# Up projection of a gated MLP: both token parts in one 512-column matmul, seven PSUM banks a tile, sums made during the products

## The chip, the cores and the metric
The kernel runs on one core of a Trainium2 chip. The metric is the time of one execution in microseconds, as the median of three runs. Engines are named as in the profile: PE multiplies matrices and writes PSUM (eight banks of 512 fp32 columns), PEld is its weight load, DVE is the vector engine, ACT the scalar engine, POOL GpSimd, SP the queue that issues most transfers.

## The reference
A decoder layer on 512 tokens of 2048 columns: layer norm, an input projection with four groups of attention heads, an output projection, a residual with layer norm, and a gated MLP. The change lies in the MLP's first half:
```python
def conv_ffn(x, w_up, conv_w, conv_b, w_down):      # x (1, 512, 2048), w_up (2048, 11264)
    S = x.shape[1]
    u, g = jnp.split(x @ w_up, 2, axis=-1)          # 5632 columns each
    gp = jnp.pad(g, ((0, 0), (CONV_WIDTH - 1, 0), (0, 0)))
    gc = conv_b
    for tap in range(CONV_WIDTH):                   # causal, width 3, along the tokens
        gc = gc + conv_w[tap] * gp[:, tap:tap + S]
    return (jax.nn.gelu(gc) * u) @ w_down
...
    h = layer_norm(DEEPNORM_ALPHA * h + mix, ln1_g[l], ln1_b[l])
    ffn = conv_ffn(h, ffn_w_up[l], ffn_conv_w[l], ffn_conv_b[l], ffn_w_down[l])
    h = layer_norm(DEEPNORM_ALPHA * h + ffn, ln2_g[l], ln2_b[l])
```

## The kernel before
Every fp32 matrix product is made of fp32r matmuls: an operand is split into a high part (a rounded copy) and a low part (what is left), and three matmuls add high x high, high x low and low x high (`PARTS`).

The up projection takes 44 tiles `f`. A tile is 128 columns of `u` and the same 128 of `g` for all 512 tokens. It is computed as a product of 2x2 blocks with seven products instead of eight (Strassen-Winograd): the blocks of the weights are halves of the 2048 rows and `u` or `g`, those of the tokens are halves of the rows and the two halves of 256 tokens. `UP` lists for each of the seven products the bank, the half of the bank, the weight operand `iw` and the token operand `ix`. A tile's rows come in two units `u` of four blocks of 128, so a unit is 7 x 4 x 3 = 84 matmuls of 256 columns.

The token operands are made once, at the stage's start, in `up_half0`, `up_half1` and `up_sums`, for eight blocks `kp`, and stay in SBUF: `xo[kp][part][ix]`. `up_first` computes tile 0 in plain form beside that.

The weight operands of a unit are made in `weight_operands`, at high precedence (an offset of 900 instructions): SP loads the blocks (`wr`), ACT makes the high parts `wh` and a negated copy in `wl`, a transfer on POOL's queue adds the weights to `wl` in memory (L926), POOL makes the four sums `S` (L934 to L937), ACT and DVE split them into `ws` (L899, L900). `wh` and `wl` have two buffers, `S` two, `ws` 12, the temporaries `t` 36. Each engine works its queue in order; the order is fixed when the program is built.

`ffn_up(f, u, n)` runs one unit of tile `f`, as its first (n = 0) or second (n = 1). The tile holds four PSUM banks (`bank4`; tags "g" with three banks and "a" with five): products 1 and 4 share a bank, 3 and 5, 2 and 6. After the second unit `up_finish` adds up: ACT copies product 0, DVE makes six adds (L996 to L1002). `gated` then does the convolution (one ACT step L1010, two DVE steps L1011 and L1013), the GELU on ACT (L1015) and the multiplication with `u` (L1016, on POOL), and every second tile `set_aside` makes token sums on POOL for the down projection and stores them. `step_aside` is called once per unit.

The order of the products is 0 to 6 from tile 5 on; in the first tiles the products with sums of tokens come last. The last two tiles run their units in another order (`up_sequence`). In tiles 2 to 17 `up_residual` takes one of 16 blocks of the residual a tile: a load, two DVE steps, a store (L1053 to L1057).

Of the kernel before, what the change touches and what calls it, by code (L numbers as in the profile page):

```python
# [11 lines left out]
F32 = mybir.dt.float32  # L12
F32R = mybir.dt.float32r
AF = mybir.ActivationFunctionType
# [3 lines left out]
P = 128  # L18
# [6 lines left out]
FT = DFF // P  # L25
# [16 lines left out]
class Trunk:  # L42
# [774 lines left out]
    def up_half0(self, kp):  # L817
        nc = self.nc
        e = self.up_blocks(kp, 0, "g")
        o = self.pT.tile([P, 2, 512], F32R, tag="T", name="x0")  # L820
        nc.gpsimd.tensor_scalar(o[:, 0], e, 1.0, 0.0, op0=ALU.mult, op1=ALU.add)
        nc.vector.tensor_sub(o[:, 1], e, o[:, 0].bitcast(F32))
        self.e0.append(e)
        self.xo.append([[o[:, p, :256], o[:, p, 256:]] for p in range(2)])

    def up_half1(self, kp):

        nc = self.nc
        e1 = self.up_blocks(kp, 1, "a")
        x12, x22 = (self.tmp(nm, (P, 2, 256), F32R) for nm in ("x12", "x22"))  # L830
        for i, x in enumerate((x12, x22)):
            e = e1[:, i * 256:(i + 1) * 256]
            nc.gpsimd.tensor_scalar(x[:, 0], e, 1.0, 0.0, op0=ALU.mult, op1=ALU.add)
            nc.vector.tensor_sub(x[:, 1], e, x[:, 0].bitcast(F32))
        self.x12.append(x12)
        self.e1.append(e1)
        for p in range(2):
            self.xo[kp][p].append(x22[:, p])

    def up_sums(self, kp):  # L840
        nc = self.nc
        e0, e1 = self.e0[kp], self.e1[kp]
        b11, b21, b12, b22 = e0[:, :256], e0[:, 256:], e1[:, :256], e1[:, 256:]
        tt = self.pP.tile([P, 4, 256], F32, tag="P", name="tt")
        nc.vector.tensor_sub(tt[:, 0], b12, b11)
        nc.gpsimd.tensor_sub(tt[:, 2], b22, b12)
        nc.vector.tensor_sub(tt[:, 1], b22, tt[:, 0])
        nc.gpsimd.tensor_sub(tt[:, 3], b21, tt[:, 1])
        if kp < 4:
            xt = [self.pT.tile([P, 4, 256], F32R, tag="T", name="xt") for _ in range(2)]  # L850
            xt = [[x[:, i:i + 2] for x in xt] for i in (0, 2)]
        else:
            xt = [[self.tmp("xt", (P, 2, 256), F32R) for _ in range(2)] for _ in range(2)]
        for i in range(2):
            nc.scalar.copy(xt[i][0], tt[:, 2 * i:2 * i + 2])
            nc.vector.tensor_sub(xt[i][1], tt[:, 2 * i:2 * i + 2], xt[i][0].bitcast(F32))
        for p in range(2):
            self.xo[kp][p] += [xt[i // 2][p][:, i % 2] for i in range(4)]

    def up_first(self):  # L860


        nc = self.nc
        ps = [self.bank("g", "up") for _ in range(2)]
        ws = [self.next_unit(), self.next_unit()]
        self.x12, self.e1 = [], []

        def products(u, half, k):
            kp = 4 * u + k
            x1 = ([self.xo[kp][p][0] for p in range(2)] if half == 0  # L870
                  else [self.x12[kp][:, p] for p in range(2)])
            x2 = [self.xo[kp][p][1 + half] for p in range(2)]
            for g, iw, x in ((0, 0, x1), (1, 3, x1), (0, 1, x2), (1, 2, x2)):
                for i, j in self.PARTS:
                    nc.tensor.matmul(
                        ps[g][:, half * 256:(half + 1) * 256],
                        ws[u][iw][i][:, k * P:(k + 1) * P], x[j],
                        start=(half == 0 and kp == 0 and iw in (0, 3) and (i, j) == (0, 0)),
                        stop=(kp == 7 and iw in (1, 2) and (i, j) == (1, 0)),
                        skip_group_check=True)  # L880

        for k in range(4):
            products(0, 0, k)
        for k in range(4):
            products(1, 0, k)
            self.up_half1(k)
        for k in range(4):
            products(0, 1, k)
            self.up_half1(4 + k)
        for kp in range(4):  # L890
            self.up_sums(kp)
        for k in range(4):
            products(1, 1, k)
            self.up_sums(4 + k)
        return ps
# [61 lines left out]
    def up_product(self, bk, w, u, i, opens, last):  # L957
        b, half, iw, ix = self.UP[i]
        ps = bk[b][:, half * 256:(half + 1) * 256]
        for k in range(4):  # L960
            x = self.xo[4 * u + k]
            for i, j in self.PARTS:
                self.nc.tensor.matmul(  # L963
                    ps, w[iw][i][:, k * P:(k + 1) * P], x[j][ix],
                    start=(opens and k == 0 and (i, j) == (0, 0)),
                    stop=(last and k == 3 and (i, j) == (1, 0)), skip_group_check=True)

    def ffn_up(self, f, u, n):

        if n == 0:  # L970
            self.bk[f] = self.bank4(f % 2 == 0, "up"), set()
        bk, opened = self.bk[f]
        w = self.next_unit()


        late = max(0, 5 - f) if u == 0 else int(f == 1)
        for i in (*range(3, 3 + late), 0, 1, 2, *range(3 + late, 7)):
            b = self.UP[i][0]
            self.up_product(bk, w, u, i, b not in opened, n == 1)
            opened.add(b)  # L980
        self.step_aside()
        if (f, n) == (FT - 1, 0):
            for kp in range(4):
                self.hidden_operands(kp)
        if n == 1:
            self.up_finish(f, self.bk.pop(f)[0])

    def up_finish(self, f, bk):
        nc = self.nc
# [15 lines left out]
    def gated(self, f, g, up):  # L1005

        nc = self.nc
        c = self.tmp("c")
        cw = lambda k: self.prm[:, C_CW + 44 * k + f:C_CW + 44 * k + f + 1]
        nc.scalar.activation(c, g, AF.Identity, bias=self.prm[:, C_CB + f:C_CB + f + 1], scale=cw(2))  # L1010
        nc.vector.scalar_tensor_tensor(c[:, 1:], g[:, :511], cw(1), c[:, 1:], op0=ALU.mult,  # L1011
                                       op1=ALU.add)
        nc.vector.scalar_tensor_tensor(c[:, 2:], g[:, :510], cw(0), c[:, 2:], op0=ALU.mult,  # L1013
                                       op1=ALU.add)
        nc.scalar.activation(c, c, AF.Gelu_apprx_tanh)  # L1015
        (nc.vector if f == 0 else nc.gpsimd).tensor_mul(c, c, up)  # L1016
        c = c.rearrange("p (a n) -> p a n", a=2)
        if f % 2 == 0:
            self.b1 = c
        else:  # L1020
            self.aside.append(self.set_aside(self.b1, c))
# [147 lines left out]
    def ffn(self):  # L1169
        nc = self.nc  # L1170
# [3 lines left out]
        for f, u in self.up_sequence():  # L1174
            n = int(f in seen)
            seen.add(f)
            if f > 0:
                self.ffn_up(f, u, n)
            elif n:
                self.gated(f, *self.up_first())  # L1180
            if n and 2 <= f < 18:
                self.up_residual(f - 2)
        self.st2 = [self.cst.tile([P, 4, 6], F32, name=f"st2_{t}") for t in range(NT)]
        self.due = deque((4, 5))
        acc = []
# [1 line left out]
        for c, k0, nk in self.CHUNKS:  # L1187
            sets = self.column_sets(c)
            for q in sets:
                bk = [self.bank("g" if i < 3 else "a", "dn") for i in range(7)]  # L1190
                nu = nk // 2
                for u in range(nu):
                    w = self.next_unit()
# [26 lines left out]
        for f in range(2, 4):  # L1220
            h, l = self.load_unit(self.wtail[f])
# [3 lines left out]
        for t in range(NT):  # L1225
            ps = self.bank("g" if t else "a", "dt")
            for f in range(8):
                x = self.ho[18 + f // 2][((0, 7), (1, 2))[f % 2][t // 2]]
                for j, p in self.PARTS:
                    nc.tensor.matmul(ps, x[j][:, t % 2 * P:(t % 2 + 1) * P], tail[f][p],  # L1230
                                     start=(f == 0 and (j, p) == (0, 0)),
                                     stop=(f == 7 and (j, p) == (1, 0)))
# [155 lines left out]
```

## Time and profile before
| | |
|---|---|
| median of 3 runs | 2337.31 us (2329.66 to 2339.68) |
| the profiled execution: its time, its span | 2341.35 us, 2339.6 us |
| PE, PEld busy in the span | 2232.7 us (95%), 2083.5 us (89%) |
| DVE, ACT, POOL busy | 1591.7 us (68%), 1229.5 us (53%), 1368.4 us (58%) |
| matmuls | 15454 |
| matmuls of up at L963, first and last start | 917.4 to 1829.3 us |
| granted clock of PE, mean | 0.983 of full speed |

Busy is the time in which an engine works on at least one instruction. Matmuls overlap: one of 256 columns lasts 283 ns in the profile, but the next begins before it ends, so the spacing of starts tells the pace. Idle time of an engine is put down to what released it ("<-").

### The profile page before, as it was taken

The page shows a single profiled execution, that of the slowest core. Times are in us where ns is not written, and L with a number is a line of the kernel's source. Part 1 is how long each engine was busy: PE and PEld are TensorE (multiplying, and loading weights), DVE is VectorE, ACT ScalarE, POOL GpSimd, SP SyncE. Part 2 cuts the span into 40 slices and gives each one's busy share as a digit, 9 for nine tenths or more (in the row PEclk, how much of TensorE's full clock was granted, in tenths as well). Part 3 has the DMA queues.
Part 4 walks back from the last instruction along what each step waited for, and adds up shares of the span by engine and source line. Part 5 has one row for each costly group of instructions (what it writes and reads, how often), then busy time and mean ns, then how long its engine had stood idle before and what let it go on. Part 6 is the DMA issues. An engine that isn't in the chain of part 4 may idle for free. (4 is left out here: it accounts for less than half of the span.)

```text
span 2339.6 us, 40306 instructions
## 1 busy us (share of the span) xinstructions
PE 2232.7 (95%) x15454; PEld 2083.5 (89%) x15454; DVE 1591.7 (68%) x2204; ACT 1229.5 (53%) x2129; POOL 1368.4 (58%) x1197
## 2 busy tenths in 40 slices
PE   7999999999999998899999999999999899999995
PEld 6788888888888878899999999999999899899994
DVE  7544455456675348687787767777676878677778
ACT  5444453355563135565555555565555666565651
POOL 5212110123234517787887878877777687777874
PEclk9999999999999999999999999999999999999998
DMA  6322223222124363888888777777778888788873
GB/s 228 92 81 73 78 67 106 84 64 62 59 88 149 104 188 94 224 226 227 231 222 238 202 210 207 201 204 197 212 202 227 243 241 233 193 229 216 207 191 115
DMA packets 125362, 392.75 MB, mean 168 GB/s; under 512 B 13632, under 2 KB 23744, under 8 KB 125168
## 3 DMA queue, kind: packets, MB, share of 16 engines
q1 hardware_dynamic: 106304, 287.72, 35.6%
q0 software_dynamic: 18720, 102.24, 24.6%
q8 instruction: 121, 1.98, 0.3%
q14 instruction: 73, 0.60, 0.1%
q10 hardware_dynamic: 144, 0.21, 0.0%
HBM read 354.36 MB, written 35.65 MB: 167 GB/s over the span
## 5 line engine op out<-in xcount | busy, mean ns | idle before, releaser
L900 DVE TENSOR_TENSOR ws<-S,ws 128x512 fp32r<-128x512 f32 x512 | 600.1, 1192 | 244.3 <-ACT ws L899 238.9
L963 PE MATMUL up<-xt,ws 128*128 128x256 f32 x3096 | 386.4, 283 | 0.3 <-DVE ws L900 0.3
L963 PEld LDWEIGHTS up<-xt,ws 128*128 128x128 f32 x3096 | 378.0, 192 | 0.6 <-DVE ws L900 0.6
L899 ACT CAST ws<-S 128x512 fp32r<-128x512 f32 x512 | 307.0, 615 | 114.9 <-POOL S L934 33.5
L100 DVE TENSOR_TENSOR wl<-wr,wh 128x1024 fp32r<-128x1024 f32 x122 | 155.2, 1272 | 213.3 <-ACT wh L99 198.4
L936 POOL TENSOR_TENSOR S<-wr 128x512 f32<-128x512 f32 x128 | 212.0, 1656 | 92.5 <-DVE ws L900 87.3
L342 POOL TENSOR_SCALAR P<-P,r 128x128 f32<-128x128 f32 (+3 forms) x144 | 81.1, 582 | 308.5 <-DVE r L337 166.2
L963 PE MATMUL up<-x,wh 128*128 128x256 f32 x1376 | 258.8, 288 | 0.0
L99 ACT CAST wh<-wr 128x1024 fp32r<-128x1024 f32 x122 | 128.0, 1049 | 233.7 <-PE op L733 78.8
L934 POOL TENSOR_TENSOR S<-wr 128x512 f32<-128x512 f32 x128 | 183.8, 1436 | 108.0 <-issue 45.3
L925 ACT ACTIVATE wl<-wr 128x512 fp32r<-128x512 f32 (+1 forms) x260 | 205.1, 836 | 67.3 <-PE dn L1115 43.5
L928 ACT CAST wh<-wr 128x512 fp32r<-128x512 f32 (+1 forms) x260 | 211.5, 829 | 35.7 <-PE up L963 33.8
L963 PE MATMUL up<-x,wl 128*128 128x256 f32 x688 | 200.8, 292 | 29.5 <-DMA wl<-in_wup_dram 29.3
L963 PEld LDWEIGHTS up<-x,wh 128*128 128x128 f32 x1376 | 220.5, 197 | 0.0
L937 POOL TENSOR_TENSOR S<-wr,S 128x512 f32<-128x512 f32 x128 | 211.8, 1655 | 0.0
L935 POOL TENSOR_TENSOR S<-S,wr 128x512 f32<-128x512 f32 x128 | 198.5, 1551 | 9.7
L1115 PE MATMUL dn<-wh,hx 128*128 128x256 f32 x792 | 157.5, 292 | 13.3 <-DVE acc L1128 8.6
L963 PEld LDWEIGHTS up<-x,wl 128*128 128x128 f32 x688 | 135.8, 197 | 33.7 <-DMA wl<-in_wup_dram 33.7
L1115 PEld LDWEIGHTS dn<-wh,hx 128*128 128x128 f32 x792 | 132.3, 200 | 14.9 <-issue 6.3
L733 PE MATMUL op<-wh,oTs 128*128 128x512 f32 x448 | 140.6, 391 | 0.0
L963 PE MATMUL up<-x,ws 128*128 128x256 f32 x1032 | 137.9, 283 | 0.0
L1015 ACT ACTIVATE c<-c 128x512 f32<-128x512 f32 x44 | 27.8, 632 | 208.0 <-DVE c L1013 208.0
(327 smaller groups left out, 5321.3 us busy)
## 6 DMA issues: line engine op xcount, KB each, us to landing
wr<-in_wup_dram SPq DMA_DIRECT2D x176, 512.0 KB
wl<-in_wup_dram POOLq DMA_DIRECT2D x88, 768.0 KB, 7.5
wr<-in_wm_dram SPq DMA_DIRECT2D x84, 512.0 KB
wr<-in_wdown_dram SPq DMA_DIRECT2D x84, 512.0 KB
wl<-in_wdown_dram POOLq DMA_DIRECT2D x42, 768.0 KB, 7.4
wr<-in_wout_dram SPq DMA_DIRECT2D x32, 512.0 KB
hid<-c SPq DMA_DIRECT2D x44, 256.0 KB
hid<-ht SPq DMA_DIRECT2D x44, 256.0 KB
```

Source lines behind the costliest of these rows:

```text
L100: nc.vector.tensor_sub(l[:, :cols], raw[:, :cols], h[:, :cols].bitcast(F32))
L733: nc.tensor.matmul(ps, ot[ct][:, a, t * P:(t + 1) * P], w[b][:, c2 * 512:(c2 + 1) * 512], start=(first and (a, b) == (0, 0)), stop=(last a ...
L899: self.nc.scalar.copy(h, raw)
L900: self.nc.vector.tensor_sub(l, raw, h.bitcast(F32))
L925: nc.scalar.mul(l3[:, o], i, -1.0)
L928: nc.scalar.copy(h3[:, o], i)
L934: nc.gpsimd.tensor_add(s12[:, 0], a21, a22)
L935: nc.gpsimd.tensor_sub(s12[:, 1], s12[:, 0], a11)
L936: nc.gpsimd.tensor_sub(s34[:, 0], a11, a21)
L937: nc.gpsimd.tensor_sub(s34[:, 1], a12, s12[:, 1])
L963: self.nc.tensor.matmul(ps, w[iw][i][:, k * P:(k + 1) * P], x[j][ix], start=(opens and k == 0 and (i, j) == (0, 0)), stop=(last and k == 3 ...
L1115: self.nc.tensor.matmul(bk[i][:, a * 256:(a + 1) * 256], x[ix][j][:, a * P:(a + 1) * P], w[iw][p][:, q * 256:(q + 1) * 256], start=first a ...
```

## The change
In tiles 1 to 41 the high weight part meets both token parts in one matmul of 512 columns: the high token part's product goes to the left half of a bank, the low part's to the right half; the low weight part adds high tokens to the left half. A product so holds a bank by itself, and a tile seven of eight. Product 3 is the exception: it keeps its three matmuls of 256 columns, all into the left half. The token operands are laid out as one view with both parts.

The sums are taken step by step while the second unit runs: a step stands in the program right behind the last product that it needs. Adding both halves of a bank takes two DVE adds, 13 of 256 columns a tile instead of six. The convolution writes its result to the eighth bank, and the GELU reads it there and writes SBUF. The residual's 16 blocks are taken in every second tile from 2 to 32. The functions `up_first`, `up_product` and the last two tiles change only the way in which they name the operands.
```diff
-        self.xo.append([[o[:, p, :256], o[:, p, 256:]] for p in range(2)])
+        self.xo.append([o[:, :, :256], o[:, :, 256:]])
...
-        for p in range(2):
-            self.xo[kp][p].append(x22[:, p])
+        self.xo[kp].append(x22)
...
-        if kp < 4:
-            xt = [self.pT.tile([P, 4, 256], F32R, tag="T", name="xt") for _ in range(2)]
-            xt = [[x[:, i:i + 2] for x in xt] for i in (0, 2)]
-        else:
-            xt = [[self.tmp("xt", (P, 2, 256), F32R) for _ in range(2)] for _ in range(2)]
         for i in range(2):
-            nc.scalar.copy(xt[i][0], tt[:, 2 * i:2 * i + 2])
-            nc.vector.tensor_sub(xt[i][1], tt[:, 2 * i:2 * i + 2], xt[i][0].bitcast(F32))
-        for p in range(2):
-            self.xo[kp][p] += [xt[i // 2][p][:, i % 2] for i in range(4)]
+            if kp < 4:
+                o = self.pT.tile([P, 2, 2, 256], F32R, tag="T", name="xt")
+                self.split_pair(tt[:, 2 * i:2 * i + 2], o[:, 0], o[:, 1])
+                self.xo[kp] += [o[:, :, k] for k in range(2)]
+            else:
+                for k in range(2):
+                    o = self.tmp("xt", (P, 2, 256), F32R)
+                    self.split_pair(tt[:, 2 * i + k], o[:, 0], o[:, 1])
+                    self.xo[kp].append(o)
...
+    def up_paired(self, bk, w, u, i, opens, last):
+        _, _, iw, ix = self.UP[i]
+        for k in range(4):
+            x = self.xo[4 * u + k][ix]
+            h, l = (w[iw][j][:, k * P:(k + 1) * P] for j in range(2))
+            if i == 3:
+                for n, (a, b) in enumerate(((h, x[:, 0]), (h, x[:, 1]), (l, x[:, 0]))):
+                    self.nc.tensor.matmul(bk[i][:, :256], a, b, start=opens and k + n == 0,
+                                          stop=last and k == 3 and n == 2, skip_group_check=True)
+                continue
+            self.nc.tensor.matmul(bk[i].rearrange("p (a n) -> p a n", a=2), h, x,
+                                  start=opens and k == 0, stop=False, skip_group_check=True)
+            self.nc.tensor.matmul(bk[i][:, :256], l, x[:, 0], start=False,
+                                  stop=last and k == 3, skip_group_check=True)
...
     def ffn_up(self, f, u, n):
+        paired = f < FT - 2
         if n == 0:
-            self.bk[f] = self.bank4(f % 2 == 0, "up"), set()
+            self.bk[f] = ([self.bank("g" if i < 3 else "a", "up") for i in range(7)] if paired
+                          else self.bank4(f % 2 == 0, "up")), set()
...
+        if paired and n == 1:
+            sums = self.up_sum_steps(f, bk)
+            done = set()
         for i in (*range(3, 3 + late), 0, 1, 2, *range(3 + late, 7)):
+            if paired:
+                self.up_paired(bk, w, u, i, n == 0, n == 1)
+                if n == 1:
+                    done.add(i)
+                    while sums and done.issuperset(sums[0][0]):
+                        sums.popleft()[1]()
+                continue
...
+    def up_sum_steps(self, f, bk):
+        nc = self.nc
+        pu, g, uu, up = self.tmp("pu"), self.tmp("g"), self.tmp("uu"), self.tmp("up")
+        lo, hi = slice(0, 256), slice(256, 512)
+        p1, u2 = pu[:, lo], pu[:, hi]
+        add = nc.vector.tensor_add
+        def step(o, i, b):
+            add(o, i, bk[b][:, lo])
+            if b != 3:
+                add(o, o, bk[b][:, hi])
+        def opening():
+            nc.scalar.copy(p1, bk[0][:, lo])
+            add(p1, p1, bk[0][:, hi])
+        def closing():
+            step(g[:, hi], uu[:, lo], 6)
+            self.gated(f, g, up)
+        return deque((
+            ((0,), opening),
+            ((0, 1), lambda: step(g[:, lo], p1, 1)),
+            ((0, 4), lambda: step(u2, p1, 4)),
+            ((0, 4, 3), lambda: step(uu[:, lo], u2, 3)),
+            ((0, 4, 5), lambda: step(uu[:, hi], u2, 5)),
+            ((0, 4, 5, 3), lambda: step(up[:, hi], uu[:, hi], 3)),
+            ((0, 4, 5, 2), lambda: step(up[:, lo], uu[:, hi], 2)),
+            ((0, 4, 3, 6), closing)))
...
     def gated(self, f, g, up):
-        c = self.tmp("c")
+        c = self.bank("a", "cv") if 0 < f < FT - 2 else self.tmp("c")
...
-        nc.scalar.activation(c, c, AF.Gelu_apprx_tanh)
+        o = self.tmp("c") if 0 < f < FT - 2 else c
+        nc.scalar.activation(o, c, AF.Gelu_apprx_tanh)
+        c = o
...
     def ffn(self):
-            if n and 2 <= f < 18:
-                self.up_residual(f - 2)
+            if n and 2 <= f < 34 and f % 2 == 0:
+                self.up_residual(f // 2 - 1)
```

## Rows read from the trace of the kernel before
**Rows 1.** Windows: stages; columns: length, busy of each engine, granted clock, DMA share, GB/s.
```profile
960.00:1300.00 340.00, 328.47 (x2681) 326.64 (x2680) 264.99 (x286) 194.58 (x305) 267.63 (x208) 0.98 0.85 230
1300.00:1790.00 490.00, 482.15 (x4000) 480.12 (x3998) 358.80 (x383) 283.64 (x449) 392.55 (x309) 1.00 0.78 205
```

**Rows 2.** Timeline of PE from 1700 us: start, length, engine, line, group, count.
```profile
1700.65 0.40 PE L963 MATMUL up<-x,wh 128*128 128x256 f32 x2
...
1702.81 0.40 PE L963 MATMUL up<-x,wh 128*128 128x256 f32 x2
```

**Rows 3.** Timeline of PE at the output projection's end.
```profile
859.75 3.56 PE L733 MATMUL op<-wres,oTs 128*128 128x512 f32 x15
```

**Rows 4.** Line L1015, 960 to 1790 us: duration in ns, first and last start.
```profile
L1015 ACT ACTIVATE c<-c x39: 630/632/634, 974.9 to 1770.7; 128x512 f32<-128x512 f32 x39
```

**Rows 5.** Waits, 960 to 1790 us: who, for whom, us in total, times, longest.
```profile
ACT c L1015 <- DVE c L1013: 197.3, 39, 6.7
...
DVE res L1054 <- DMA res<-res: 49.1, 15, 5.2
...
PE up L963 <- DMA wl<-in_wup_dram: 19.3, 18, 4.5
```

**Rows 6.** Windows of L963: length, PE and PEld busy, granted clock, DMA share, GB/s.
```profile
1080.00:1100.00 20.00, 15.49 (x116) 15.29 (x115) 0.86 0.85 238
...
1260.00:1280.00 20.00, 17.09 (x121) 16.89 (x121) 0.83 0.92 237
```

**Rows 7.** Line L926, 960 to 1790 us: its transfers.
```profile
DMA to landing us min/median/max: 6.5/7.3/11.7
```

**Rows 8.** Timeline of PE at a tile's end.
```profile
1450.96 1.60 PE L963 MATMUL up<-x,ws 128*128 128x256 f32 x12
1452.40 0.40 PE L963 MATMUL up<-x,wh 128*128 128x256 f32 x2
```

**Rows 9.** Timeline of DVE at the same tile's end.
```profile
1450.83 0.93 DVE L900 TENSOR_TENSOR ws<-S,ws 128x512 fp32r<-128x512 f32 x1
...
1452.28 1.18 DVE L900 TENSOR_TENSOR ws<-S,ws 128x512 fp32r<-128x512 f32 x1
1453.38 0.41 DVE L999 TENSOR_TENSOR g<-uu,up 128x256 f32<-128x256 f32 x1
1453.72 0.41 DVE L1001 TENSOR_TENSOR up<-uu,up 128x256 f32<-128x256 f32 x1
1454.05 3.49 DVE L900 TENSOR_TENSOR ws<-S,ws 128x512 fp32r<-128x512 f32 x1
...
1457.79 1.72 DVE L1011 SCALAR_TENSOR_TENSOR c<-g,prm,c 128x511 f32<-128x511 f32 x1
1459.54 1.67 DVE L1013 SCALAR_TENSOR_TENSOR c<-g,prm,c 128x510 f32<-128x510 f32 x1
```

**Rows 10.** Timeline of ACT after it; in brackets the idle time before.
```profile
1461.30 0.63 ACT L1015 ACTIVATE c<-c 128x512 f32<-128x512 f32 x1 [6.66 <-DVE c L1013]
...
1462.35 1.58 ACT L925 ACTIVATE wl<-wr 128x512 fp32r<-128x512 f32 x2
```

**Rows 11.** Timeline of POOL after it: the transfer's issue.
```profile
1465.92 0.86 POOL L926 DMA_DIRECT2D wl<-in_wup_dram  x1
```

**Rows 12.** Timeline of PE in the output projection, between attention's matmuls.
```profile
710.53 0.62 PE L733 MATMUL op<-wh,oTs 128*128 128x512 f32 x2
710.99 0.40 PE L733 MATMUL op<-wl,oTs 128*128 128x512 f32 x1
711.22 0.62 PE L733 MATMUL op<-wh,oTs 128*128 128x512 f32 x2
```

**Rows 13.** Groups of DVE by form, 880 to 960 us: count, busy us, mean ns.
```profile
L834 DVE TENSOR_TENSOR x<-ev,x 128x256 fp32r<-128x256 f32 x16 | 9.3, 588 | 3.6 <-POOL x L833 3.6
L822 DVE TENSOR_TENSOR x<-ev,x 128x512 fp32r<-128x512 f32 x8 | 7.2, 936 | 0.0
...
L751 DVE SCALAR_TENSOR_TENSOR acc<-acc,op 128x512 f32<-128x512 f32 x1 | 0.7, 674 | 0.0
```

**Rows 14.** Timeline of DVE, another tile's end.
```profile
1411.99 3.57 DVE L900 TENSOR_TENSOR ws<-S,ws 128x512 fp32r<-128x512 f32 x1
1415.48 0.41 DVE L999 TENSOR_TENSOR g<-uu,up 128x256 f32<-128x256 f32 x1
```

More of the change, by code (lines that the diff above doesn't have):

```diff
@@ L869, in products @@
             kp = 4 * u + k
-            x1 = ([self.xo[kp][p][0] for p in range(2)] if half == 0
-                  else [self.x12[kp][:, p] for p in range(2)])
-            x2 = [self.xo[kp][p][1 + half] for p in range(2)]
+            x1, x2 = self.xo[kp][0] if half == 0 else self.x12[kp], self.xo[kp][1 + half]
             for g, iw, x in ((0, 0, x1), (1, 3, x1), (0, 1, x2), (1, 2, x2)):
@@ L876, in products @@
                         ps[g][:, half * 256:(half + 1) * 256],
-                        ws[u][iw][i][:, k * P:(k + 1) * P], x[j],
+                        ws[u][iw][i][:, k * P:(k + 1) * P], x[:, j],
                         start=(half == 0 and kp == 0 and iw in (0, 3) and (i, j) == (0, 0)),
@@ L963, in up_product @@
                 self.nc.tensor.matmul(
-                    ps, w[iw][i][:, k * P:(k + 1) * P], x[j][ix],
+                    ps, w[iw][i][:, k * P:(k + 1) * P], x[ix][:, j],
                     start=(opens and k == 0 and (i, j) == (0, 0)),
                     stop=(last and k == 3 and (i, j) == (1, 0)), skip_group_check=True)
+    def up_paired(self, bk, w, u, i, opens, last):
[12 more added lines that the diff above has]
+                                  stop=last and k == 3, skip_group_check=True)
     def ffn_up(self, f, u, n):
+        paired = f < FT - 2
         if n == 0:
-            self.bk[f] = self.bank4(f % 2 == 0, "up"), set()
+            self.bk[f] = ([self.bank("g" if i < 3 else "a", "up") for i in range(7)] if paired
+                          else self.bank4(f % 2 == 0, "up")), set()
         bk, opened = self.bk[f]
@@ L985, in ffn_up @@
         if n == 1:
-            self.up_finish(f, self.bk.pop(f)[0])
+            if paired:
+                del self.bk[f]
+            else:
+                self.up_finish(f, self.bk.pop(f)[0])
+    def up_sum_steps(self, f, bk):
[23 more added lines that the diff above has]
+            ((0, 4, 3, 6), closing)))
     def up_finish(self, f, bk):
```

## The prediction
> **What bounds the kernel now.** I read the views from wide to narrow. The table by stages comes first [rows 1]: from 960 to 1300 us and from 1300 to 1790 us, where tiles of the up projection follow each other, TensorE is busy 97% and 98% of the time, the other engines 57 to 80%. So in the up stage PE sets the pace, and the rest of the kernel is touched by no edit. Next the spacing of the matmuls. Seven triples of up begin between 1700.65 and 1702.81, six steps of 0.36 us [rows 2]: 120 ns for each 256-column matmul. Of 512 columns, 15 begin within 3.56 - 0.39 us [rows 3], 226.5 ns each. As a line through both: 0.416 ns a column and 13.5 ns for each matmul, whatever its width. That fixed part is what the change can save.
>
> A tile is 168 matmuls, 20.16 us. The 39 GELUs of the stage begin between 974.9 and 1770.7 us [rows 4], 20.94 us apart. So 0.78 us a tile, 29.7 us over 38 tiles, is not matmul. The waits say what it is [rows 5]: PE waits 18 times, 19.3 us, for `wl`, the low weight part that a POOL transfer completes. After two of them (4.5 and 2.9 us, the idle time in two stretches of 20 us) the clock fell for a time from 2.4 to 1.2 GHz: the granted clock is 0.86 and 0.83 of full in these stretches [rows 6], 2.8 + 3.4 us more.
>
> Why is `wl` late? The transfer takes 7.3 us at the median [rows 7], so the delay stands before it. At one tile's end PE finishes at 1452.40 [rows 8]. DVE adds `g` at 1453.38, is then held for 3.49 us by one split of a weight sum, and runs the two convolution steps until 1461.2 [rows 9]. ScalarE has stood before its GELU for 6.66 us [rows 10], 197.3 us over 39 tiles [rows 5]; the casts and the `wl` preparation of the next weights are queued behind it. POOL issues the transfer at 1465.92 [rows 11], it lands some 7 us later, and PE wants it two units after 1452.40, at about 1472.6. There is no slack in that round.
>
> **Part by part.**
> *Pairing.* Three matmuls of 256 columns (360 ns) become one of 512 and one of 256 (226.5 + 120 = 346.5 ns). The saving is 13.5 ns, for 41 tiles x 2 units x 6 products x 4 blocks = 1968 pairs: **26.6 us**. Product 3 stays as it is. The low end: where the out projection runs between other work, three 512-column matmuls take 0.69 us, from 710.53 to 711.22 [rows 12], 230 ns each; then it is 19.7 us. I take 26.6, since up runs as dense as the stretch of [rows 3]. The moving operand is now two runs of 256 columns instead of one of 512; no row has that form, and I charge nothing (the weight operand and the bank are as before).
> The Trainium skill ("TensorE: Matmul & The Clock Gate", Back-to-back issue gap) puts the gap at columns / 2.4 plus 2.5 ns. By it the saving would be 1968 x 2.5 ns, an estimate of 4.9 us. The rows show 13.5 ns and decide; the rule is kept as a rival below.
>
> *Convolution in PSUM.* The two DVE steps read `g` and `c` from SBUF and take 1.72 and 1.67 us [rows 9] beside POOL's work. The same operation with one input from PSUM took 0.674 us [rows 13]. GELU, and all that is queued behind it, comes 2 x 1.7 - 2 x 0.67 = **2.0 us** sooner. The bounds are 0 and 2.0, since the write also moves to PSUM and no row shows that; I take 2.0.
>
> *Weight waits.* `wl` comes 2.0 us sooner. It is wanted sooner too: between its buffer's release and its need lie 11 products, each 54 ns shorter, 0.6 us. That leaves 1.4 us. Of 18 waits of 1.07 us on average the short ones go and the two long ones keep 3.1 and 1.5; some 12 of 19.3 us go, and one of the two falls of the clock (3.4). I take **-15 us**; the ends are 0 and 19.3 + 6.2 = 25.5.
>
> *Residual spread.* The 16 residual steps stay, but two tiles apart, down to f = 32. In each, DVE stood some 3.3 us before the load (49.1 us in 15, [rows 5]), all of it between 960 and 1300 us, where PE idles most (11.5 of 340 us against 7.9 of 490, [rows 1]). They will block as often, but never in two tiles running. I count no gain beyond the 15 us; if the waits only move to the second half, part of the 15 is lost, which the lower bound 0 holds.
>
> *Sums.* Six adds a tile (five of 256 columns, one of 512) become 13 of 256. An add takes 0.41 us and the next begins after 0.34 [rows 9]: 13 x 0.34 = 4.4 us against 2.3, 2.1 more, about what the convolution gives back. DVE was 78% and 73% busy in the two stretches [rows 1]; over a tile of 19.5 us instead of 20.9 the same work is some 81%. The cover is this idle time. Where it ends is the next part.
>
> *Seven banks.* Before, a tile takes four of eight banks and the next tile the others, so the final adds have a whole tile of time. Now seven banks hold one tile and the eighth `c`, and the next tile's product i begins in the bank of this tile's product i. Most are read long before. Bank 2 isn't: its two adds stand behind products 4 and 5, and the next tile wants it after products 6, 0 and 1, 3 x 1.386 = 4.16 us after product 5 ends. Between lie five adds, one after the other 5 x 0.41 = 2.05 us. That leaves 2.1 us, enough for one ordinary split of 1.2 us (the one at 1452.28, [rows 9]) that gets ahead of them. It isn't enough for the long one. In the tile shown it lasts 3.49 us [rows 9] and comes behind `g`. In another it lasts 3.57 us, at 1411.99, ahead of `g` at 1415.48 [rows 14]. Of the six tiles between 1388 and 1508 us it came ahead in two. Where it gets ahead of bank 2's adds: 0.8 us of a split in progress (the one at 1450.83, [rows 9], against product 5's end at 1450.96, [rows 8]) + 3.57 + 2.05 = 6.4, a stall of about 2.3 us. The bounds are none and all 41 tiles (94 us). I take five tiles, **+11 us**: a third of the tiles have it early, and of these it must also fall within the five adds.
>
> The new adds wait for the ends of products, in DVE's queue. Behind them stand the next splits, for which POOL's weight sums and so its next transfer wait; the split that follows each product is itself due only when that product has ended, so I charge nothing where the queue runs in step, and what a DVE that falls behind costs is rival (a). The four temporaries of the sums are taken a unit earlier than before: of 36 buffers 24 hold token operands, and these four, two `c`, two `ht` and three of the residual make 11 of the 12 left. It fits by one buffer, so nothing is charged; if it didn't, ScalarE's first copy would wait for it, which (a) and (b) hold too.
>
> *Start of the stage.* For four of eight blocks the token sums are split in 16 pieces of 256 instead of 8 of 512. DVE: 16 x 0.588 - 8 x 0.936 [rows 13] = 1.9 us more; bounds 0 and 1.9, I take 1, as ScalarE's work partly covers it.
>
> Sum: -26.6 - 15 + 11 + 1 = -29.6 us. Against the profiled execution's 2341.35 us that is 2311.8; the median of the runs shown, 2337.31, lies 4.0 lower: **2308 us**, 1.3% faster.
>
> **Rivals.**
> (a) *Slower: bank 2 comes late.* The place is the wait of the next tile's product 2 on DVE; the price 2.3 us a tile. With the other terms at -40.6 us it breaks even at 18 tiles; from 23 it is slower by 0.5%. In 33 of 41 tiles it costs 76 us: 2373. For it: DVE's queue is in order and its weight splits were given precedence, the long split comes in every tile, and a stall shifts PE onto the next one. Against it: in two thirds of the tiles seen the long split comes after the last product.
> By the Trainium skill (the same page, A second HAM failure mode: psum-queue depth-cycling), cycling through PSUM banks with small pauses makes the clock go up and down; the trace has falls only after the two longest waits [rows 5, 6], and if stalls of 2.3 us did the same, (a) would cost more still.
> (b) *No change: weights pace the stage.* PE ends sooner and waits for `wl` what it gained, since POOL is busy 79 to 80% and DMA 78 to 85% of the time [rows 1]. Against it: in the second stretch PE idles only 7.9 us in some 24 tiles, though ScalarE stands 6 us in each. Time: 2337 if all is lost, 2323 if half is; some 2330.
> (c) *All waits go.* With the GELU early enough nothing is late: -26.6 - 25.5 + 1 = -51, 2286.
> (d) *The fixed part isn't saved,* as by the page's formula: -5 - 15 + 11 + 1 = -8, 2329.
>
> **How the numbers follow.** Chances: the forecast 0.48, (a) 0.18, (b) 0.14, (c) 0.14, (d) 0.06. The likeliest one's own range is 2285 to 2332 (the waits gained 0 to 25, the stalls 0 to 25). Leaving out the upper two thirds of (a) and the low edge of (c), 8 in 10 lie between **2283 and 2345**. A change below 0.5% (11.7 us) is about what a measurement can't tell from none. Faster than 2325.6: 0.45 of the forecast, all of (c), a fifth of (b), half of (d): 0.65. Slower than 2349: most of (a): 0.16. The rest, 0.19.
>
> **What would show it.** In the profile after: up's matmuls as 512 then 256 columns, 0.3465 us a pair; 19.5 to 20.2 us between GELUs; the convolution steps near 0.7 us; ScalarE's standing before the GELU down from 5 us to about 3; PE's wait for `wl` under 10 us in all; a new wait of PE for DVE's add of bank 2, five or so times about 2 us. It would be wrong if the pair takes 0.36 us (d), if that new wait comes in most tiles (a), or if the wait for `wl` grows by what the matmuls saved (b).

## The result and the profile after

The changed kernel takes 2442.68 us (median; 2440.38 to 2444.3), the kernel before 2336.56 in the same comparison: a ratio of 1.046 [1.0431, 1.049], slower by 4.6%. The span grew from 2339.6 to 2438.6 us. The forecast was 2308; rival (a), bank 2 late, happened, and dearer than it was priced. One execution of the experiment with another order of the products ran at a granted clock of 0.75 and took 2704.22 us; the median given for it below, 2362.1 us, is that of its other three.

The GELUs of the up stage, as count, shortest/median/longest ns and first and last start:
```profile
L1081 ACT ACTIVATE c<-cv x41: 583/589/601, 960.0 to 1888.7; 128x512 f32<-128x512 f32 x41
```
Before, the same 41 began from 956.7 to 1792.2, 20.9 us apart. Now they are 23.2 us apart; the last is 96.5 us late, so nearly all of the 99 us of the span is lost in these tiles. Next the windows, which answer to [rows 1] and [rows 6] (columns as there):
```profile
960.00:1300.00 340.00, 305.31 (x1789) 267.35 (x1787) 241.96 (x350) 180.07 (x282) 238.92 (x194) 0.97 0.74 196
1300.00:1790.00 490.00, 433.27 (x2496) 379.07 (x2497) 338.54 (x500) 253.79 (x398) 336.94 (x270) 0.95 0.73 192
1790.00:1880.00 90.00, 82.67 (x480) 72.65 (x479) 61.02 (x93) 48.78 (x76) 63.32 (x53) 0.96 0.72 188
...
1200.00:1220.00 20.00, 14.25 (x78) 12.63 (x79) 7.22 (x10) 6.93 (x12) 7.62 (x7) 0.78 0.50 123
1520.00:1540.00 20.00, 17.05 (x97) 14.95 (x96) 15.17 (x21) 8.21 (x14) 16.36 (x14) 0.92 0.85 228
```
Every engine is less busy than before: PE 90% and 88% instead of 97% and 98%, and DVE fell too. So no engine became the bound; they wait for each other. The granted clock is 0.97, 0.95 and 0.96: against full speed 340 x 0.03 + 490 x 0.05 + 90 x 0.04 = some 38 us, against some 7 before. In windows of 0.5 us, 12 of the 38 lie in pauses of PE, where a low clock costs nothing more (1 of the 7 before); so some 26 us against some 6 were lost in matmuls. The clock falls from 2.4 to 1.2 GHz for a time not only after a long wait for weights (0.78) but also in stretches that hold only pauses at banks (0.92).

The waits between 960 and 1880 us, which answer to [rows 5] (engine and line, what released it: us in total, times, longest):
```profile
DVE ws L898 <- ACT ws L897: 229.1, 156, 4.7
ACT wh L926 <- PE up L978: 168.1, 80, 3.6
ACT cv L1075 <- DVE g L1031: 163.5, 39, 6.8
POOL wl L924 <- ACT wl L923: 163.4, 40, 13.4
...
PE up L978 <- DVE up L1031: 60.9, 30, 3.3
...
PE up L980 <- DMA wl<-in_wup_dram: 33.6, 8, 9.7
...
PE up L978 <- DVE pu L1035: 3.5, 3, 1.3
...
PE up L978 <- DVE g L1031: 0.8, 2, 0.4
```
PE's waits are the ones to read, since PE sets the pace: 60.9 us in 30 waits for DVE's second add of a bank (L1031), with the other two rows 65.2 us. None of these stands in the same view of before. The wait for `wl` grew from 19.3 us in 18 waits [rows 5] to 33.6 in 8, of up to 9.7 us. ScalarE no longer stands before the GELU; it stands before the first convolution step, 163.5 us (50.3 before).

What one such pause looks like on PE, and what DVE and POOL did just before it:
```profile
1485.15 0.40 PE L978 MATMUL up<-x,ws 128*128 128x512 f32 x1
...
1489.39 1.12 PE L975 MATMUL up<-xt,ws 128*128 128x256 f32 x8
1493.45 0.50 PE L978 MATMUL up<-xt,wh 128*128 128x512 f32 x1 [2.94 <-DVE up L1031]
```
```profile
1485.05 0.41 DVE L1029 TENSOR_TENSOR pu<-pu,up 128x256 f32<-128x256 f32 x1
1485.49 0.42 DVE L1031 TENSOR_TENSOR pu<-pu,up 128x256 f32<-128x256 f32 x1
1485.83 1.13 DVE L898 TENSOR_TENSOR ws<-S,ws 128x512 fp32r<-128x512 f32 x1
1486.88 0.41 DVE L1029 TENSOR_TENSOR uu<-pu,up 128x256 f32<-128x256 f32 x1
1487.21 3.14 DVE L898 TENSOR_TENSOR ws<-S,ws 128x512 fp32r<-128x512 f32 x1
1490.28 0.41 DVE L1029 TENSOR_TENSOR uu<-pu,up 128x256 f32<-128x256 f32 x1
1490.61 0.41 DVE L1029 TENSOR_TENSOR g<-uu,up 128x256 f32<-128x256 f32 x1
1490.94 0.68 DVE L898 TENSOR_TENSOR ws<-S,ws 128x512 fp32r<-128x512 f32 x1
1491.54 0.41 DVE L1031 TENSOR_TENSOR uu<-uu,up 128x256 f32<-128x256 f32 x1
1491.87 0.41 DVE L1031 TENSOR_TENSOR g<-g,up 128x256 f32<-128x256 f32 x1
1492.20 0.74 DVE L1029 TENSOR_TENSOR up<-uu,up 128x256 f32<-128x256 f32 x2
1492.98 0.42 DVE L1031 TENSOR_TENSOR up<-up 128x256 f32<-128x256 f32 x1
1493.32 0.75 DVE L1076 SCALAR_TENSOR_TENSOR cv<-g,prm,cv 128x511 f32<-128x511 f32 x1
```
```profile
1487.05 1.50 POOL L934 TENSOR_TENSOR S<-wr 128x512 f32<-128x512 f32 x1
1488.31 1.49 POOL L935 TENSOR_TENSOR S<-wr,S 128x512 f32<-128x512 f32 x1
1491.75 1.27 POOL L932 TENSOR_TENSOR S<-wr 128x512 f32<-128x512 f32 x1 [1.96 <-issue]
```
Product 6 begins at 1485.15, so product 5 has just ended; PE reaches the place of the next tile's product 2 at 1489.39, 4.24 us later. Product 2 (`xt,wh`) begins when bank 2's last add (1492.98) is done. From 1485.05 to the end of that add DVE needs 8.35 us, for three weight splits (1.13, 3.14 and 0.68 us) and ten adds: those of products 4, 3 and 5, both adds of `g` from product 6, which finished last, and bank 2's own two. The long split runs while POOL makes two weight sums, the shortest in the gap behind them. PE has run all that it could, two thirds of product 3 among it. In another tile, at 1514.52, the same pause is 0.98 us; the split in that place takes 1.68 us there.

The pairs, as PE starts them:
```profile
1509.60 0.40 PE L978 MATMUL up<-x,wh 128*128 128x512 f32 x1
1509.84 0.28 PE L980 MATMUL up<-x,wl 128*128 128x256 f32 x1
...
1512.43 1.12 PE L975 MATMUL up<-xt,ws 128*128 128x256 f32 x8
```
Eight pairs lie between 1509.60 and 1512.43: 0.354 us each, of which the wide matmul takes some 0.235. Three matmuls took 0.360 [rows 2].

### The profile page after: what moved, and what is told of

Its sections match the earlier page's. It is cut to its first block, busy times and chain, and to the rows that moved or that the text cites. A ratio compares the mean times of both kernels' runs of the same rounds, so it can differ in the third digit from the quotient of the medians.

```text
span 2438.6 us, 36870 instructions
## 1 busy us (share of the span) xinstructions
PE 2243.7 (92%) x13486; PEld 1991.3 (82%) x13486; DVE 1610.3 (66%) x2499; ACT 1233.5 (51%) x2137; POOL 1341.2 (55%) x1197
## 5 line engine op out<-in xcount | busy, mean ns | idle before, releaser
L898 DVE TENSOR_TENSOR ws<-S,ws 128x512 fp32r<-128x512 f32 x512 | 581.5, 1146 | 364.2 <-ACT ws L897 326.6
L926 ACT CAST wh<-wr 128x512 fp32r<-128x512 f32 (+1 forms) x260 | 212.2, 832 | 171.8 <-PE up L978 168.1
L978 PE MATMUL up<-x,wh 128*128 128x512 f32 x656 | 244.0, 409 | 4.2 <-DVE pu L1035 3.5
L932 POOL TENSOR_TENSOR S<-wr 128x512 f32<-128x512 f32 x128 | 181.6, 1419 | 104.5 <-issue 61.3
L978 PE MATMUL up<-xt,ws 128*128 128x512 f32 x656 | 238.8, 403 | 0.0
L934 POOL TENSOR_TENSOR S<-wr 128x512 f32<-128x512 f32 x128 | 189.5, 1481 | 78.6 <-DVE ws L898 70.3
L924 POOL DMA_DIRECT2D wl<-in_wup_dram x88 | 77.2, 877 | 237.6 <-ACT wl L923 221.1
L978 PE MATMUL up<-xt,wh 128*128 128x512 f32 x328 | 131.2, 431 | 61.0 <-DVE up L1031 60.9
L980 PE MATMUL up<-xt,ws 128*128 128x256 f32 x656 | 185.6, 283 | 0.0
L933 POOL TENSOR_TENSOR S<-S,wr 128x512 f32<-128x512 f32 x128 | 180.4, 1409 | 8.5
L978 PEld LDWEIGHTS up<-x,wh 128*128 128x128 f32 x656 | 127.2, 194 | 36.8 <-issue 4.5
L978 PEld LDWEIGHTS up<-xt,ws 128*128 128x128 f32 x656 | 125.6, 191 | 27.2
```

The lines of the kernel that those rows point to most:

```text
L898: self.nc.vector.tensor_sub(l, raw, h.bitcast(F32))
L926: nc.scalar.copy(h3[:, o], i)
L932: nc.gpsimd.tensor_add(s12[:, 0], a21, a22)
L933: nc.gpsimd.tensor_sub(s12[:, 1], s12[:, 0], a11)
L934: nc.gpsimd.tensor_sub(s34[:, 0], a11, a21)
L978: self.nc.tensor.matmul(bk[i].rearrange("p (a n) -> p a n", a=2), h, x, start=opens and k == 0, stop=False, skip_group_check=True)
```

## The experiments

The theory after this reading: DVE's queue holds bank 2, PE pauses there and the clock falls. Its rival: the loss comes from elsewhere (late weights, temporaries, the convolution's eighth bank), and the waits at the banks only take up time that would be lost anyway. Unless said otherwise an edit is made to the changed kernel, "waits" are PE's in the up matmuls from 960 to 1880 us, and a ratio is to the kernel before on the same chip. That kernel's median was 2332.52 to 2342.05 us beside the four groups of experiments, so times from different groups are compared by what is "lost" against it: 106 us for the changed kernel.

**Bank 2 read early.** Its two halves are added right after its product, by a copy on ScalarE and an add on DVE, and joined later in SBUF:
```diff
+        def second():
+            nc.scalar.copy(up[:, lo], bk[2][:, lo])
+            add(up[:, lo], up[:, lo], bk[2][:, hi])
...
+            ((0, 1, 2), second),
...
-            ((0, 4, 5, 2), lambda: step(up[:, lo], uu[:, hi], 2)),
+            ((0, 4, 5, 2), lambda: add(up[:, lo], up[:, lo], uu[:, hi])),
```


> The changed kernel, but bank 2 is read as soon as product 2 ends (a ScalarE copy of its left half, a DVE add of its right half); the sum with product 5 is added later in SBUF. Theory 1 (bank 2's late release holds PE: 30 waits, 61 us, and most of the clock's falls, 38 us in all): PE's wait for DVE's adds of bank 2 falls under 5 us, the time to 2345 to 2375 us. Theory 2 (the round of the weights sets the tile, the wait at bank 2 only shows it first): the wait moves to the low weight part and the time stays above 2420 us.


2390.74 us, 1.0202 [1.0185, 1.0218]. 49 us are lost: 57 of the 106 went, less than expected. PE still waits 36.4 us, now for bank 5's second add, right behind the next tile's product 3, and 13.8 for the early add of bank 2 itself. Of the 13.8, 11.8 are three waits of 3.3 to 5.1 us in every eighth tile, behind a DVE that had stood up to 6.5 us for the residual's load. So it is the order of DVE's queue more than the one bank.

**A spare bank.** The convolution goes back to SBUF; the bank so freed rotates with those of products 2, 4, 5 and 6:
```diff
-        self.bk[f] = ([self.bank("g" if i < 3 else "a", "up") for i in range(7)] ...
+        self.bk[f] = ([self.bank("g" if i in (0, 1, 3) else "a", "up") for i in range(7)] ...
...
-        c = self.bank("a", "cv") if 0 < f < FT - 2 else self.tmp("c")
+        c = self.tmp("c")
```


> The changed kernel with the convolution back in SBUF and the eighth bank given to the group of product 2, so that the next tile's product 2 begins in a bank that has been free for long. Theory 1: PE's wait for bank 2 goes, the time falls to 2350 to 2385 us though the two convolution steps take 1.7 instead of 0.75 us again. Theory 2: the GELU and with it the next weights come some 2 us later, so the time is 2440 us or more.


2350.49 us, 1.0036 [1.0018, 1.0054]. 8 us are lost: one spare bank, with the convolution's move, gives back 98 us. The waits are 30.8 us in 32, none over 1.5 us, now for the bank of product 3, and the clock is 0.99 and 1.00. This speaks against the rival: with shorter pauses the stage runs. The waits for `wl` fall as well, to 4.3 us.

**Three matmuls again.** The pair becomes two matmuls of 256 columns and one:
```diff
-            self.nc.tensor.matmul(bk[i].rearrange("p (a n) -> p a n", a=2), h, x,
+            for a in range(2):
+                self.nc.tensor.matmul(bk[i][:, a * 256:(a + 1) * 256], h, x[:, a],
...
```


> The changed kernel, seven banks and sums as they are, but each 512-column matmul made as two of 256 (three matmuls of 256 columns a block again). The pairs ran at 0.354 us against 0.360 us for three. Theory 1: PE's own work grows by 1968 x 6 ns = 12 us, most of it beside the stalls: 2443 to 2456 us, and the wait at bank 2 shrinks a little, since the three products before it take 0.07 us longer. Theory 2: PE isn't the pace, 2443 us within 3. If pairs had saved the forecast 13.5 ns, 2460 to 2470 us.


2428.32 us, 1.0364 [1.0344, 1.0384]: 86 us are lost, 20 fewer than with pairs, where more were expected. The waits at banks grew to 72.9 us, but the long ones for `wl` are gone. So the pairs can't be priced where other waits move; a later pair of runs does it.

**Sums at the end of the program's tile.** All steps are placed behind the last product:
```diff
-                    while sums and done.issuperset(sums[0][0]):
-                        sums.popleft()[1]()
...
+                for _, step in sums:
+                    step()
```


> The changed kernel with all sums placed behind the last product, as before the change. Theory 1: every bank is then late, the next tile's product 0 waits for the copy and the adds as well, 1.5 to 3 us a tile more: 2500 to 2560 us. Theory 2: the weights still pace the tile: 2443 us within 15.


2441.63 us, 1.0419 [1.0394, 1.0444], with 59.6 us of waits at banks: the same as the changed kernel (their intervals overlap). "Sums made as products end", as a place in the program, does nothing; the order on DVE, which is fixed when the program is built, comes out alike: at the tile's end that was shown it is the same, operation by operation.

**Rows of their own.** Every eighth tile `up_residual` loads two rows of the layer norm into temporaries. Here they get two other buffers:
```diff
-        t = self.tmp(name)
+        t = (self.cst.tile([P, 512], F32, tag="bias", name=name, bufs=2) if own
+             else self.tmp(name))
```


> The changed kernel, but the two broadcast rows that the residual loads every eighth tile lie in two buffers of their own, not among the 36 temporaries. Theory: the three waits of 9 to 10 us for the low weight part come every eighth tile because the rows and the four sums together use up the temporaries, so that ScalarE's first copy of a tile stands in a late place. Then they go (33.6 us to under 6), some falls of the clock too: 2395 to 2412 us. Rival: they come from the weights' round itself, 2440 us within 6.


2407.57 us, 1.0328 [1.0303, 1.0353]: 75 us are lost, 31 fewer. The waits for `wl` fall from 33.6 to 4.3 us, as expected; those for banks stay (66.6). In the changed kernel the long chain starts where the rows are loaded:
```profile
1343.41 0.49 SPq L84 DMA_DIRECT2D g<-in_rows_dram  x1
1343.99 0.45 SPq L84 DMA_DIRECT2D b<-in_rows_dram  x1
```
```profile
1370.34 0.78 ACT L1075 ACTIVATE cv<-g,prm 128x512 f32<-128x512 f32 x1 [6.80 <-DVE g L1031]
```
```profile
1376.57 0.88 POOL L924 DMA_DIRECT2D wl<-in_wup_dram  x1 [6.43 <-ACT wl L923]
...
1388.86 0.86 POOL L924 DMA_DIRECT2D wl<-in_wup_dram  x1
```
```profile
1397.28 0.58 PE L980 MATMUL up<-x,wl 128*128 128x256 f32 x1 [9.70 <-DMA wl<-in_wup_dram]
```
A tile later ScalarE stands 6.80 us before the convolution, the casts behind it are late, POOL's issue of `wl` waits 6.43 us for them, the next one stands behind POOL's own work, and PE waits 9.70 us.

**Another order of the products.** In the second unit product 3 comes after 5, so that bank 2's adds can be made one product sooner (the expectation says two); the sums follow that order:
```diff
-        for i in (*range(3, 3 + late), 0, 1, 2, *range(3 + late, 7)):
+        for i in ((0, 1, 2, 4, 5, 3, 6) if paired and n == 1 and late == 0 else
+                  (*range(3, 3 + late), 0, 1, 2, *range(3 + late, 7))):
...
```


> The changed kernel with the products of a tile's second unit in the order 0, 1, 2, 4, 5, 3, 6, and the sums in the order of their products: bank 2 and bank 3 are then complete two products sooner, which gives DVE one product more before the next tile wants them. Theory 1 (bank 2's release costs): the wait of 61 us falls to about 15, 2370 to 2400 us. Theory 2 (the weights' round costs): 2430 us or more.


2362.1 us, 1.0132 [1.0109, 1.0154], better than expected: 30 us are lost. The waits at banks are 38.9 us in 23, and those for `wl` are 4.8 without any change to the rows. But the trouble of every eighth tile isn't gone: three of the 23 take 6.1 to 7.5 us, 20.3 together, and in front of them DVE stands for the residual's load:
```profile
1512.35 0.69 DVE L1122 SCALAR_TENSOR_TENSOR res<-res,g 128x512 f32<-128x512 f32 x1 [5.49 <-DMA res<-res]
```
```profile
1519.55 0.77 PE L978 MATMUL up<-xt,wh 128*128 128x512 f32 x1 [6.06 <-DVE up L1032]
```
With the rows apart as well (the last experiment) no wait at a bank is over 1.9 us.

**The residual alone.** The kernel before, with the residual in every second tile:
```diff
-            if n and 2 <= f < 18:
-                self.up_residual(f - 2)
+            if n and 2 <= f < 34 and f % 2 == 0:
+                self.up_residual(f // 2 - 1)
```


> The kernel before with the residual spread over the even tiles 2 to 32 and nothing else changed. By the prediction the DVE waits before the residual never fall in two tiles running: 0 to 8 us saved, 2330 to 2340 us. Rival: the waits only move to the second half, within 3 us of the kernel before.


2335.36 us, 1.0015 [0.9997, 1.0034]. No effect.

**Spare bank, order and rows together,** with the convolution in SBUF:

> The changed kernel with the rows apart, the product order 0, 1, 2, 4, 5, 3, 6, the convolution back in SBUF and the eighth bank given to the group of product 2. If late banks and used-up temporaries are the whole loss, nothing holds PE but a few waits for weights: 41 tiles of 19.9 us, 2300 to 2330 us, faster than both kernels. If the weights' round sets a tile of 20.5 us or more, 2335 us or more.


2351.85 us, 1.008 [1.0051, 1.0108]: a miss: 19 us are lost, no fewer than with the spare bank alone (8). The waits at banks are still 34.0 us. What is left isn't a shortage of banks alone.

**Sums first.** The adds get precedence over the weight splits when DVE's order is fixed:
```diff
-            add(o, i, bk[b][:, lo])
-            if b != 3:
-                add(o, o, bk[b][:, hi])
+            with self.tc.high_priority(offset=1500):
+                add(o, i, bk[b][:, lo])
+                if b != 3:
+                    add(o, o, bk[b][:, hi])
...
```


> The changed kernel with the sums (ScalarE's copy and DVE's 13 adds) given precedence over the weight splits when DVE's order is fixed; nothing else is moved. Theory 1 (the splits that stand ahead of the adds hold bank 2): between product 5's adds and bank 2's last add stands one split where two stood; the wait falls from 61 us to 20 to 35, the time to 2390 to 2415 us, the three long waits for weights still there. Theory 2 (the weights' round is what costs): the splits come later, so 2443 us or more.


2392.96 us, 1.025 [1.0227, 1.0273]: 58 us are lost, with 49.8 us of waits at banks. The time is in the range of theory 1, the wait is longer than it said, and of the three long waits for `wl` one of 3.6 us is left.

**Three matmuls with rows apart; convolution in SBUF with rows apart.** Edits as above, two at a time.

> The kernel of rows apart (2407.6 us) with three matmuls of 256 columns in place of a pair: the price of the pair alone, without the long waits that came and went in the run with three matmuls before. The pairs ran at 0.354 us, three at 0.360: 1968 x 6 ns = 12 us, 2408 to 2420 us, less where the stalls take it up. Rival: the wider matmul itself makes something late, since the other run with three matmuls was 14 us faster: under 2403 us.


2411.54 us, 1.0332 [1.0311, 1.0353]: 77 us are lost against 75 with pairs, no difference clear of noise.

> The kernel of rows apart (2407.6 us) with the convolution back in SBUF; the eighth bank stays in the group of products 3 to 6. If the convolution in PSUM pays, as forecast: its two steps take 1.7 instead of 0.75 us, the GELU and the weights behind it come 2 us later a tile, 2415 to 2435 us. Rival: the bank is worth more than the 2 us, as the next products find it free: 2400 us or less.


2387.11 us, 1.0235 [1.0198, 1.0273], where the rival to the forecast had put it: 52 us are lost instead of 75. Where banks are scarce the eighth bank is worth more than quick steps; the profile, of an execution of 2400.55 us, has 57.3 us of waits at banks instead of 66.6.

**Order, sums first and rows apart together,** the convolution in PSUM as in the change:

> The changed kernel with rows apart, the product order 0, 1, 2, 4, 5, 3, 6 and the sums given precedence; convolution in PSUM. Theory 1: bank 2 and 3 have one product more and one split less ahead, PE's waits for banks fall under 10 us: 2305 to 2335 us, as fast as the kernel before or faster. Theory 2: ScalarE still stands before the convolution and the weights are late: 2345 us or more, the wait moved to the low weight part.


2310.0 us (2309.32 to 2312.52), 0.9899 [0.9876, 0.9922]: 1.0% faster than the kernel before, and with the 106 us that the changed kernel lost, 131 better than that. Its windows, and from 950 to 1800 us its only wait of PE (4.3 us from 960 on):
```profile
960.00:1300.00 340.00, 335.71 (x2019) 296.95 (x2018) 278.96 (x402) 205.36 (x321) 272.24 (x220) 0.99 0.87 222
1300.00:1780.00 480.00, 480.00 (x2967) 428.74 (x2967) 388.50 (x563) 294.51 (x463) 387.81 (x313) 1.00 0.89 224
```
```profile
ACT cv L1079 <- DVE g L1034: 106.0, 40, 3.0
...
PE up L981 <- DMA wl<-in_wup_dram: 9.5, 3, 5.2
```
DVE at a tile's end (line numbers are higher by 3: L1032 and L1034 are the two adds, L899 the split), and PE's first matmul of product 2:
```profile
1514.99 0.41 DVE L1032 TENSOR_TENSOR up<-uu,up 128x256 f32<-128x256 f32 x1
1515.32 0.41 DVE L1032 TENSOR_TENSOR uu<-pu,up 128x256 f32<-128x256 f32 x1
1515.66 0.41 DVE L1034 TENSOR_TENSOR up<-up 128x256 f32<-128x256 f32 x1
1515.99 0.41 DVE L1032 TENSOR_TENSOR up<-uu,up 128x256 f32<-128x256 f32 x1
1516.32 0.41 DVE L1032 TENSOR_TENSOR g<-uu,up 128x256 f32<-128x256 f32 x1
1516.65 1.61 DVE L899 TENSOR_TENSOR ws<-S,ws 128x512 fp32r<-128x512 f32 x1
1518.18 0.41 DVE L1034 TENSOR_TENSOR g<-g,up 128x256 f32<-128x256 f32 x1
```
```profile
1518.19 0.40 PE L979 MATMUL up<-xt,wh 128*128 128x512 f32 x1
```
Bank 2's last add ends at 1515.66 + 0.41 = 1516.07, 2.1 us before PE wants the bank. The long split now comes behind it and harms nobody.

**Three controls on that version:** three matmuls, convolution in SBUF, and without the precedence.

> The fastest version (2310.0 us) with three matmuls of 256 columns in place of a pair. PE is busy without a gap there, so the pair shows its price: at 0.354 against 0.360 us 1968 x 6 ns = 12 us, 2318 to 2326 us. If the forecast's 13.5 ns held, 2333 to 2340 us. If weights pace the tile, within 3 us of 2310.


2326.64 us, 0.9964 [0.9947, 0.998]. 16.6 us more by the medians, 15 by the ratios. PE is busy in all of the 450 us from 1300 to 1750 in both kernels, so this is the price of the pairs with little else moving.

> The fastest version with the convolution back in SBUF, the eighth bank in the group of products 3 to 6. If a free bank is worth more than a short convolution only where banks are late, this is now the other way round: the steps take 1.7 instead of 0.75 us, the weights behind the GELU come later, 2313 to 2335 us. If the convolution's place has no weight in a kernel that PE sets, 2310 us within 4.


2315.15 us, 0.9932 [0.991, 0.9953]: 5 us more by the medians, 8 by the ratios, hardly clear of noise (the intervals touch), with 10.0 us of waits at banks.

> The fastest version without the precedence of the sums: rows apart and the product order alone. The product order alone left a bank wait of 39 us and 2363 us. If the rows add what they did on the changed kernel (35 us), 2325 to 2340 us; if precedence is what frees the banks, the wait stays near 39 us, 2345 to 2365 us.


2352.72 us, 1.0077 [1.005, 1.0104], with 26.5 us of waits at banks in 21. So the order alone leaves 38.9 (26.5 with rows apart), the precedence alone 49.8, and both with rows apart none: with either alone something still stands ahead of a bank's add in some tiles. The precedence with rows apart, and both without them, weren't run.

## Why the prediction was wrong

| term | forecast, us | measured, us |
|---|---|---|
| pairing | -26.6 | -12 by the spacing of pairs; -15 to -17 by experiment |
| weight waits and their clock | -15 | +14 (33.6 against 19.3), clock in the row below |
| pauses at the banks | +11 | +65.2 |
| clock | within the two above | +20 in matmuls (26 against 6) |
| start of the stage | +1 | +3 (first GELU 960.0 against 956.7) |
| sum | -29.6 | +90, where the last GELU came 96.5 us later; some 6 us stay open |

**The step that failed is the seven banks.** It counted "five adds" and one split between product 5's end and the need of bank 2, and took five tiles. The rows above show three splits and ten adds there, 8.35 us where 4.16 were to be had, and in the whole stage 30 waits and 60.9 us; even in the other tile, whose longest split takes 1.68 us, PE stops for 0.98. The closing adds of product 6, the last product, stood ahead of bank 2's. The argument also took the share of tiles from the kernel before ("of the six tiles ... two"), in which DVE's order was made for other adds. The slack that decided between "fits" and "doesn't" was 2.1 us, smaller than the spread of one instruction there: two of the splits in the rows above took 3.14 and 0.68 us. Rival (a) had the place and the sign. Its 76 us of stalls for 33 tiles is near the 65.2 measured, though not for its reasons: 16 pauses took 2.5 to 3.3 us and 14 some 0.7 to 1.0. What it left out of its price is the clock, which it named: after eight of the 16 long pauses the clock fell, and with the falls after the waits for weights that cost another 20 us in matmuls. The order with precedence took pauses and falls away together (clock 0.99 and 1.00), and the spare bank, which left pauses of at most 1.5 us, shows 0.99 and 1.00 too. The Trainium skill ("TensorE: Matmul & The Clock Gate", A second HAM failure mode: psum-queue depth-cycling) tells of a bf16 kernel whose small pauses between banks make the clock go up and down; with the clock at 0.95 to 0.97 here, the trace agrees, though pauses up to 1.5 us did without.

**A second step failed: "it fits by one buffer, so nothing is charged".** In every eighth tile two rows of the layer norm are loaded into the same 36 buffers; the count has no such tile. Then the convolution, the casts and two transfers came late, and PE waited up to 9.7 us three times; buffers of their own gave back 31 us. That the chain starts with a buffer that isn't free is inferred from that run; no view shows the wait for a buffer by name. Where other edits took the long waits for `wl` away, the late tile mostly showed elsewhere: with bank 2 read early, the other order or the precedence DVE stood 15.8 to 21.1 us in all for the residual's load, and with rows apart 1.6 us or less in every version with the convolution in PSUM. With three matmuls (4.5 us for `wl`, none over 3.4 at a bank) and with the spare bank the long waits went altogether, so they also depend on when the other engines run.

**Weight waits, -15:** they didn't go. The convolution steps became as fast as forecast (0.75 us for two steps that took 1.72 and 1.67, [rows 9]; 0.67 was expected), and yet ScalarE stands 163.5 us, a place earlier, instead of 197.3 [rows 5] and 50.3 in the two places, since `g` itself is late. In the version with order and precedence it is 106.0, and PE's wait for `wl` 4.3, under the 10 of the forecast.

**Pairing, -26.6:** the mechanism is right, the size wrong. The line through two widths gave 226.5 ns for 512 columns; next to a 256-column matmul it takes 235, so a pair saves 6 ns instead of 13.5: 1968 x 6 = 12 us. With PE without pauses the experiment gives 16.6, 8.4 ns a pair (15 and 7.7 by the ratios). The rule of 2.5 ns a matmul (the Trainium skill, the same page, Back-to-back issue gap), which the page gives for a matmul by itself and not for a stream with weight loads, is an estimate of 4.9 us by the forecast's working and too small as well; the measurement lies between.

**Convolution in PSUM:** at most a gain of 5 to 8 us where banks are free in time (2315.15 against 2310.0, hardly clear of noise), a loss of some 20 where they aren't. The forecast priced the steps, not the bank.

**Residual and place of the sums:** nothing, as forecast for the first and shown for both (ratio 1.0015; 2441.63 against 2442.68). DVE did stop waiting for the residual's load in the changed kernel (4.4 us against 49.1, [rows 5]), but in a stage that was late anyway; in the kernel before, spread alone, it waited 61.5.

With both failed steps mended, the run stands at 2310.0. That this is near the forecast's 2308 is luck in part: the forecast had some 11 us too much for the pairs and charged 11 for pauses at banks that this version doesn't have, and the version has an order and a precedence that the change had not.

What stays open: some 6 us of the table, why the early reading of bank 2 leaves 36 us at bank 5, and what the three versions near 2351 (spare bank, all three, order with rows) lose beyond their 26 to 34 us at banks.

## What to carry to other kernels

When the banks for a tile go from four of eight to seven, work out for each bank when it is wanted again, and count everything that can stand ahead of its last reader in the in-order queue: other reads of the same tile and unrelated work of the longest duration seen, not the usual one. Slack of one instruction isn't slack: choose the order of the products so that the bank wanted first is read first, and give its readers precedence in that queue; here neither was enough without the other, as far as they were run. Count shared buffers in the worst tile, with what is loaded only now and then. Count a low clock only where the engine works: in its pauses it is already paid for.

## What the runs showed of the hardware

A matmul of 512 columns takes some 0.235 us of PE next to one of 256 (0.354 less 0.120), against 0.2265 in a run of its own kind [rows 3]. DVE's split of two SBUF operands of 512 columns takes 0.68 us in one place, where POOL stands, and 3.14 in another 4 us earlier, beside two weight sums of POOL, while its adds that read a bank keep to 0.41 and the convolution step to 0.75. After eight of the 16 pauses of 2.5 to 3.3 us at bank 2 PE's matmuls ran at 1.2 GHz for some 3 to 6 us; after the 14 of 0.7 to 1.0 us none did.
